# Three moves in the order of a hybrid decoder layer on one core: the decay stage against the first products of the pairs, the logarithms against the exponentials, and which PSUM bank three stages take first

## The chip, the cores and the metric

The kernel runs on one core of a Trainium2 chip. The metric is device time in microseconds. A core has five engines that work side by side, each through its own queue in program order: TensorE multiplies matrices (PE in the profile, with PEld for its loads of the stationary operand), VectorE (DVE) and ScalarE (ACT) work on elements, GpSimd (POOL) does a few operations on elements, and SyncE (SP) issues the transfers between HBM and the on-chip memory SBUF. Matrix products land in PSUM, of whose banks the kernel uses eight, each 128 partitions by 512 float32. An engine waits for another by semaphore.

## The reference

One layer of a decoder with two token mixers side by side. The input x has 1024 rows of 1024. What is computed, cut to its core:

```python
h = rmsnorm(x, norm_g)
proj = h @ w_in
(g_q, g_k, g_v, g_gate, g_rank,
 s_q, s_k, s_v, s_gate, m_logits) = jnp.split(proj, SPLIT_IDX, axis=-1)
log_a = jax.nn.log_sigmoid((g_rank @ w_dec_up + b_dec).astype(jnp.float32)) / GLA_TAU
o_gla = gla_chunked(g_q, g_k, g_v, log_a)          # 4 heads, chunks of 64
...
bcum = jnp.cumsum(la, axis=3)                      # in each chunk
qe = qc * jnp.exp(bcum) * (dk ** -0.5)
ke = kc * jnp.exp(-bcum)
...
o_sb = stick_breaking(s_q, s_k, s_v)               # 8 heads
y_a = (rmsnorm(o_gla, gla_norm_g) * silu(g_gate)) @ w_pa
y_b = (o_sb * silu(s_gate)) @ w_pb
merged = gates[0] * y_a + gates[1] * y_b           # gates = sigmoid(m_logits + b_gate)
return rmsnorm(x + merged @ w_o, final_g)
```

The decay is the part between `g_rank` (16 columns of the projection) and the two tables exp(bcum) and exp(-bcum), of four heads with 128 channels by 1024 tokens each.

## The kernel before

Every product of float32 is made of three: an operand is split into a high half, rounded to the format in which TensorE runs at full rate, and a low half, the difference; high by high, high by low and low by high are added up in PSUM. `split` (L160, L161) is two operations: ScalarE copies to the high half, VectorE subtracts to get the low half. In the names of the profile these are `wh` and `wl` (or `dh` and `dl`).

The projection is cut into jobs of 256 columns of the weights, and each job is computed with seven block products in place of eight (`pair_job`). A job has a load of the weights (L235, 1 MB, on SyncE's queue, into `raw`), four subtractions of GpSimd (L239 to L242) that make the sums T1 to T4 of weight blocks in the single buffer `tt`, four splits (B11 and B21; T2 and T1; B22; T3 and T4), and seven units. A unit is one product: twelve matmuls (L265 to L267) of 512 columns. The seven products use three banks "pp", called x, y and z. Units 0, 2, 4 and 6 go onto x, unit 1 onto y, units 3 and 5 onto z. Between them the banks are read: ScalarE copies x away after units 0 and 2 and z after unit 3 (`keep`, L271), and VectorE adds such a copy to a bank at units 1, 4 and 5 (`evict`, in `total` L304). So unit 4 cannot begin before ScalarE has copied x after unit 2, and unit 6 not before VectorE has made the addition of unit 4.

`Pairs.run(n)` (L79) issues the next n units of all jobs in one row: it issues the split that is due (the current job's last one at unit 0, the next job's others at units 2, 4 and 6), at unit 1 the load of the job after next, and then the unit. Units are counted here through all jobs from 0, so that unit 13 is unit 6 of the second job.

Ahead of the pairs stands the v stage (L676 to L678): 56 items of six matmuls with a row of constants of their own, with four banks `vx` (two of the tag "z" and two of the tag "tr", L660) that the items take in turn. Just ahead of it the column constants are transposed into a "tr" bank (`vcol_ps`, L156) and copied out by VectorE (L157). Two later stages have four such banks `xa` and `xb`.

The decay stage runs between the first units of the pairs, in a list `djobs` (L804): one entry of decay operations, then `pairs.run(1)`. For half the tokens `code` (L769) transposes the codes on TensorE into a "tr" bank and ScalarE (L706) and VectorE (L708) split them. For a head `logit` is two matmuls into "tr" banks (L776) with an addition by VectorE each (L777); `decay_a` (VectorE, L781) takes the negative magnitude, `decay_b` (ScalarE, L784) its exponential, `decay_c` (ScalarE, L787) the logarithm of one plus that, `decay_d` (VectorE, L790) a subtraction, `decay_e` (VectorE, L793) the running sum in chunks as a scan, `decay_f` (ScalarE, L796 and L797) two exponentials, and `decay_g` (VectorE, L800, and two stores, L801 and L802) hands the tables over. An operation on a head is 128 by 1024. Between exponential and logarithm ScalarE loads another table of functions (ACT_TABLE_LOAD). The list has 23 entries, the first of them empty.

The stage is under a manual schedule for ScalarE and VectorE: these two keep the order in which the code is written, while TensorE, GpSimd and SyncE are put in order by the planner. Behind the decay stage 40 units run with a list `tjobs` beside them (L841): loads, sums and stores of matrices for later (`t_load`, L829 and L832), at places counted from the start of that list.

## Time and profile before

| | |
|---|---|
| runs of before | 1189.11, 1189.91, 1189.92 us; median 1189.91 |
| the profiled execution's own time | 1189.16 us |
| its span | 1187.5 us |
| mean granted clock of TensorE in it | 0.995 of full speed |
| TensorE busy | 1165.4 us in 5811 matmuls |
| VectorE, ScalarE, GpSimd busy | 861.3, 553.6, 248.1 us |
| v stage starts, first unit of the pairs starts | 44.27 us, 102.64 us |
| first transposes of the codes, last exponential of the decay stage | 105.41 us, 175.79 us |

The profile is of one execution. Its span runs from the first to the last instruction; what lies around it, 1.7 us, is in the time and not in the span. Busy time is summed over all instructions of an engine, so a wait shows as the difference to the span. A row of the timeline has the start, the duration, the engine, the line, and what is written from what; in brackets stands how long the engine had been idle and which instruction released it.

### The profile page before, as it was taken

The numbers are of one execution on the slowest core, as the hardware profiler recorded it, in microseconds if no ns is written. First come the engines' busy times: TensorE is split into PE (matmuls) and PEld (weight loads), VectorE is DVE, ScalarE is ACT, GpSimd is POOL, SyncE is SP. The second block draws the span as 40 slices with busy tenths as digits, with TensorE's granted clock in tenths as the row PEclk, the third lists the DMA queues.
The fourth block names the chain that finished last, engine by engine and source line by source line (L and its number), as shares of the span: only waits on it lengthen the run. The fifth ranks groups of instructions, "written<-read, shape, count | busy, mean of one in ns | idle before, by whom it ended". The sixth has DMA issues, their size and how long they took to land.

```text
span 1187.5 us, 16606 instructions
## 1 busy us (share of the span) xinstructions
PE 1165.4 (98%) x5811; PEld 979.8 (83%) x5811; DVE 861.3 (73%) x1440; ACT 553.6 (47%) x1040; POOL 248.1 (21%) x217
## 2 busy tenths in 40 slices
PE   8999799999999999999999999999999999999997
PEld 7998678888888888888888887888888888888886
DVE  6797666787677777777666677447687876488986
ACT  6554562333454454454444443344444544364543
POOL 1022323234233233233233223000000000700001
PEclk9999999999999999999999999999999999999999
DMA  7324439998266565564444357899766646848652
GB/s 287 125 62 160 150 139 318 335 319 284 100 191 196 166 225 193 165 195 143 142 159 134 107 163 228 259 309 330 237 214 225 202 150 199 291 152 284 221 195 106
DMA packets 189455, 239.23 MB, mean 201 GB/s; under 512 B 12438, under 2 KB 128172, under 8 KB 187836
## 3 DMA queue, kind: packets, MB, share of 16 engines
q1 hardware_dynamic: 188796, 237.13, 60.3%
q8 instruction: 45, 0.74, 0.3%
q10 hardware_dynamic: 576, 1.05, 0.2%
q14 instruction: 38, 0.31, 0.1%
HBM read 150.06 MB, written 88.08 MB: 201 GB/s over the span
## 4 chain that ended last, share of the span: by engine, by line
PE 89%; DVE 4%; ACT 2%; DMA 2%; issue 1%; SPq 0%; ACTq 0%; DVEq 0%
PE pp L265 16%; PE pp L267 16%; PE pp L266 16%; PE pp L199 3%; PE pp L200 3%; PE pp L201 3%; PE pp L218 2%; PE av L1106 1%; PE av L1105 1%; PE tr L1083 1%; PE av L1104 1%; PE z L1065 1%; PE z L1067 1%; PE z L1066 1%; PE xb L1472 1%
## 5 line engine op out<-in xcount | busy, mean ns | idle before, releaser
L265 PE MATMUL pp<-S,wh 128*128 128x512 f32 x372 | 147.3, 396 | 0.7 <-ACT f L271 0.7
L267 PE MATMUL pp<-S,wl 128*128 128x512 f32 x372 | 145.0, 390 | 0.0
L266 PE MATMUL pp<-S,wh 128*128 128x512 f32 x372 | 144.9, 390 | 0.0
L161 DVE TENSOR_TENSOR wl<-tt,wh 128x1024 fp32r<-128x1024 f32 x62 | 76.5, 1234 | 56.6 <-ACT wh L160 56.2
L304 DVE TENSOR_TENSOR f<-pp,f 128x512 f32<-128x512 f32 x93 | 64.1, 689 | 71.7 <-PE pp L267 64.9
L239 POOL TENSOR_TENSOR tt<-raw 128x512 f32<-128x512 f32 x31 | 45.3, 1463 | 267.3 <-DVE wl L161 244.2
L160 ACT ACTIVATE wh<-tt 128x1024 fp32r<-128x1024 f32 x62 | 65.6, 1058 | 74.7 <-PE pp L266 66.0
L271 ACT ACTIVATE f<-pp 128x512 f32<-128x512 f32 x93 | 55.1, 592 | 89.2 <-PE pp L267 85.9
L1071 DVE TENSOR_TENSOR_SCAN be<-be,m 128x128 f32<-128x128 f32 (+3 forms) x64 | 86.2, 1349 | 6.2 <-ACT be L1068 6.1
L160 ACT ACTIVATE wh<-raw 128x1024 fp32r<-128x1024 f32 (+1 forms) x47 | 48.4, 1030 | 83.6 <-PE pp L266 46.4
L265 PEld LDWEIGHTS pp<-S,wh 128*128 128x128 f32 x372 | 70.6, 190 | 15.6 <-ACT f L271 1.6
L267 PEld LDWEIGHTS pp<-S,wl 128*128 128x128 f32 x372 | 69.8, 188 | 14.9
L266 PEld LDWEIGHTS pp<-S,wh 128*128 128x128 f32 x372 | 69.9, 188 | 13.7
L161 DVE TENSOR_TENSOR wl<-raw,wh 128x1024 fp32r<-128x1024 f32 (+1 forms) x47 | 65.2, 1388 | 16.6 <-ACT wh L160 16.1
L226 POOL TENSOR_TENSOR r<-r,nhalf 128x1 f32<-128x1 f32 x40 | 25.2, 629 | 194.2 <-DVE r L225 194.2
L1068 ACT ACTIVATE be<-z 128x384 f32<-128x384 f32 (+4 forms) x96 | 47.0, 495 | 24.0 <-PE z L1067 20.6
L1255 POOL TENSOR_TENSOR N<-A,A 128x512 f32<-128x512 f32 x4 | 6.6, 1659 | 242.9 <-DMA A<-d_osb 242.9
L265 PE MATMUL pp<-ha22h,wh 128*128 128x512 f32 x124 | 49.8, 402 | 6.3 <-DVE f L304 6.3
L267 PE MATMUL pp<-ha22h,wl 128*128 128x512 f32 x124 | 49.3, 397 | 0.0
L266 PE MATMUL pp<-ha22l,wh 128*128 128x512 f32 x124 | 49.2, 397 | 0.0
L265 PE MATMUL pp<-ha11h,wh 128*128 128x512 f32 x124 | 49.1, 396 | 0.0
L265 PE MATMUL pp<-ha12h,wh 128*128 128x512 f32 x124 | 49.0, 395 | 0.0
(528 smaller groups left out, 3394.6 us busy)
## 6 DMA issues: line engine op xcount, KB each, us to landing
raw<-in_w_in_dram SPq DMA_DIRECT2D x31, 1024.0 KB, 6.3
d_t<-t SPq DMA_DIRECT2D x16, 512.0 KB, 5.5
d_ogl<-o SPq DMA_DIRECT2D x64, 128.0 KB, 2.5
d_q<-o SPq DMA_DIRECT2D x16, 512.0 KB, 3.2
d_k<-o SPq DMA_DIRECT2D x16, 512.0 KB, 4.7
d_v<-o SPq DMA_DIRECT2D x32, 256.0 KB, 2.4
k<-d_k SPq DMA_DIRECT2D x8, 1024.0 KB, 6.1
v<-d_v SPq DMA_DIRECT2D x16, 512.0 KB, 5.4
```

The costliest lines, as they stand in the source:

```text
L160: nc.scalar.activation(hi, src, AF.Copy)
L161: eng.tensor_sub(lo, src, hi.bitcast(F32))
L199: nc.tensor.matmul(pt, whi[:, kb], h_, start=kb == 0, stop=False)
L200: nc.tensor.matmul(pt, whi[:, kb], l_, start=False, stop=False)
L239: nc.gpsimd.tensor_sub(t1, b[:, 0, 1], b[:, 0, 0])
L265: nc.tensor.matmul(pt, bh[:, j], ah[:, j], start=first and j == 0, stop=False, skip_group_check=True)
L266: nc.tensor.matmul(pt, bh[:, j], al[:, j], start=False, stop=False, skip_group_check=True)
L267: nc.tensor.matmul(pt, bl[:, j], ah[:, j], start=False, stop=j == 3, skip_group_check=True)
L271: nc.scalar.activation(t[nm], t[bank], AF.Copy)
L304: nc.vector.tensor_add(add, bank, add)
L1068: nc.scalar.activation(om[:, off + pc * w:off + (pc + 1) * w], zt[:, 0:w], AF.Sigmoid, scale=-inv_sqrt)
L1071: nc.vector.tensor_tensor_scan(rest, rest, m1[:, off:T][:, ::-1], 1.0, op0=ALU.mult, op1=ALU.max)
```

## The change

`Pairs.run` takes a list `mid` of further operations, which it issues behind the split and the load that are due and ahead of the unit. The decay stage hands its entries over in this way, where it called them itself ahead of `pairs.run(1)`. The list loses its empty first entry, so the first transposes of the codes come with the first unit, and in each half the second head's exponential and both heads' logarithms share one entry, where the logarithms had one of their own. So the list has 20 entries in place of 23. The list `tjobs` behind it becomes 43 entries long in place of 40, and its operations start three entries later, which leaves them at the same units. Three stages take the two "tr" banks ahead of the two "z" banks.

```diff
@@ class Pairs
-    def run(self, n=None):
+    def run(self, n=None, mid=()):
...
             if u == 1 and i + 2 < len(self.jobs):
                 self.jobs[i + 2]["load"]()
+            for fn, arg in mid:
+                fn(arg)
             due = self.late.pop(0) if self.late else None
             self.jobs[i]["unit"](u)
@@ hybrid_layer
-    vx = [ps.tile([P, HALF], F32, tag=tag, name="vx")[:, 0:VH] for tag in ("z", "z", "tr", "tr")]
+    vx = [ps.tile([P, HALF], F32, tag=tag, name="vx")[:, 0:VH] for tag in ("tr", "tr", "z", "z")]
...
-    djobs = [[], [(code, 0)], [(code, 1)]]
+    djobs = [[(code, 0)], [(code, 1)]]
     for h in (0, 2):
-        djobs += [[(logit, h)], [(logit, h + 1), (decay_a, h)], [(decay_b, h), (decay_a, h + 1)], [(decay_b, h + 1)],
-                  [(decay_c, h), (decay_c, h + 1)], [(decay_d, h)], [(decay_e, h), (decay_d, h + 1)],
+        djobs += [[(logit, h)], [(logit, h + 1), (decay_a, h)], [(decay_b, h), (decay_a, h + 1)],
+                  [(decay_b, h + 1), (decay_c, h), (decay_c, h + 1)], [(decay_d, h)], [(decay_e, h), (decay_d, h + 1)],
                   [(decay_f, h), (decay_e, h + 1)], [(decay_f, h + 1), (decay_g, h)], [(decay_g, h + 1)]]
...
     for jobs in djobs:
-        for fn, h in jobs:
-            fn(h)
-        pairs.run(1)
+        pairs.run(1, jobs)
...
     for k in range(8):
-        at = 4 * k
+        at = 4 * k + 3
...
-    xa = [ps.tile([P, HALF], F32, tag=tag, name="xa") for tag in ("z", "z", "tr", "tr")]
+    xa = [ps.tile([P, HALF], F32, tag=tag, name="xa") for tag in ("tr", "tr", "z", "z")]
...
-    xb = [ps.tile([P, HALF], F32, tag=tag, name="xb") for tag in ("z", "z", "tr", "tr")]
+    xb = [ps.tile([P, HALF], F32, tag=tag, name="xb") for tag in ("tr", "tr", "z", "z")]
```

The lines of the kernel after the change lie two further down from the second addition in `run` to the list `djobs`.

What ScalarE has in a row at the second exponential of the first two heads, before. `e_1349` and `e_1372` are the two heads' tables; `f_1431` is the copy of unit 6's bank, `dh_1415` the high half of B22 of the second job, and `wh_1436` that of its T3 and T4.

```order
L784 ACTIVATE e_1372<-e_1372 128x1024
L160 ACTIVATE dh_1415<-raw_1160 128x512
L566 ACTIVATE f_1431<-pp_1277 128x512
L787 ACT_TABLE_LOAD
L787 ACTIVATE e_1349<-e_1349 128x1024
L787 ACTIVATE e_1372<-e_1372 128x1024
L160 ACTIVATE wh_1436<-tt_1162 128x1024
```

The same place on ScalarE after the change, where the two heads' tables are `e_1335` and `e_1357`, the high halves `dh_1417` and `wh_1437`, and the copy of unit 6's bank `f_1434`.

```order
L786 ACTIVATE e_1357<-e_1357 128x1024
L789 ACT_TABLE_LOAD
L789 ACTIVATE e_1335<-e_1335 128x1024
L789 ACTIVATE e_1357<-e_1357 128x1024
L162 ACTIVATE dh_1417<-raw_1160 128x512
L568 ACTIVATE f_1434<-pp_1285 128x512
L162 ACTIVATE wh_1437<-tt_1162 128x1024
```

The table load and both logarithms have moved ahead of the small high half and of the copy of unit 6's bank.

Further on in ScalarE's queue, at the second exponentials of the same two heads (L796 and L797), before. `f_1453`, `f_1496` and `f_1514` are the copies of the banks of units 7, 9 and 10; `wh_1480` and `wh_1521` are high halves of the third job.

```order
L271 ACTIVATE f_1453<-pp_1440 128x512
L160 ACTIVATE wh_1480<-raw_1300 128x1024
L271 ACTIVATE f_1496<-pp_1440 128x512
L796 ACT_TABLE_LOAD
L796 ACTIVATE e_1349<-u_1348 128x1024
L797 ACTIVATE u_1348<-u_1348 128x1024
L271 ACTIVATE f_1514<-pp_1501 128x512
L796 ACTIVATE e_1372<-u_1371 128x1024
L797 ACTIVATE u_1371<-u_1371 128x1024
L160 ACTIVATE wh_1521<-tt_1302 128x1024
```

The same place after the change; the copies of the banks of units 7, 9 and 10 are `f_1456`, `f_1504` and `f_1522`, and the high halves `wh_1483` and `wh_1524`.

```order
L273 ACTIVATE f_1456<-pp_1443 128x512
L798 ACT_TABLE_LOAD
L798 ACTIVATE e_1335<-u_1334 128x1024
L799 ACTIVATE u_1334<-u_1334 128x1024
L162 ACTIVATE wh_1483<-raw_1300 128x1024
L798 ACTIVATE e_1357<-u_1356 128x1024
L799 ACTIVATE u_1356<-u_1356 128x1024
L273 ACTIVATE f_1504<-pp_1443 128x512
L273 ACTIVATE f_1522<-pp_1509 128x512
L162 ACTIVATE wh_1524<-tt_1302 128x1024
```

The exponentials of both heads now stand ahead of the copies of the banks of units 9 and 10, where the first head's stood between these two copies and the second head's behind them.

On TensorE at the start of the v stage, before: first matmuls of the second, third and fourth item. A wait for VectorE's semaphore stands in brackets as DVE_49; the bank of `vcol_ps` is that of the item which has it.

```order
L678 MATMUL vx_706<-wh_651,ha11l_209 128x384
L676 MATMUL vx_707<-wh_651,ha11h_208 128x384 [waits PE_49]
L677 MATMUL vx_707<-wl_652,ha11h_208 128x384
L678 MATMUL vx_707<-wh_651,ha11l_209 128x384
...
L678 MATMUL vx_707<-wh_651,ha11l_209 128x384
L676 MATMUL vx_708<-wh_651,ha11h_208 128x384 [waits DVE_49]
```

The same items after the change.

```order
L680 MATMUL vx_705<-wh_651,ha11l_209 128x384
L678 MATMUL vx_706<-wh_651,ha11h_208 128x384 [waits DVE_49]
L679 MATMUL vx_706<-wl_652,ha11h_208 128x384
L680 MATMUL vx_706<-wh_651,ha11l_209 128x384
```

The wait for VectorE's copy of the column constants has moved from the fourth item to the second, twelve matmuls earlier.

## The prediction

> **What bounds the kernel now.** I read the page first, then the stretches of 25 us, then the list of what each engine waited for, and last the engines' rows around the largest wait.

> ```profile
> span 1187.5 us, 16606 instructions
> PE 1165.4 (98%) x5811; PEld 979.8 (83%) x5811; DVE 861.3 (73%) x1440; ACT 553.6 (47%) x1040; POOL 248.1 (21%) x217
> PE 89%; DVE 4%; ACT 2%; DMA 2%; issue 1%; SPq 0%; ACTq 0%; DVEq 0%
> 125.00:150.00 25.00, 18.74 (x76) 14.79 (x75) 17.85 (x15) 13.10 (x15) 9.83 (x4) 0.92 0.43 165
> PE pp L265 <- DVE f L304: 6.3, 1, 6.3
> ```

> TensorE works through 98% of the span, and the chain that ended last is its own for 89%. So an edit counts by what it does to TensorE's waits and to its clock. Only 22 us are idle, and one wait holds 6.3 of them. It falls in the stretch 125 to 150 (a row of the stretches gives the length, then the busy time of PE, PEld, DVE, ACT and POOL, the granted clock, the DMA share and GB/s). Between the first stretch and the last 12 us it is the only one in which TensorE is busy for less than 20 of 25 us, and the granted clock is down to 0.92. It holds the decay stage. In the rows below a start is followed by a duration, and in brackets stand the wait ahead and its releaser.

> ```profile
> 123.55 0.39 PE L265 MATMUL pp<-ha11h,wh 128*128 128x512 f32 x1
> 126.27 0.39 PE L265 MATMUL pp<-ha12h,wh 128*128 128x512 f32 x1
> 140.17 0.61 PE L776 MATMUL tr<-rst,o 128*128 128x512 f32 x2
> 147.04 0.79 PE L265 MATMUL pp<-ha22h,wh 128*128 128x512 f32 x1 [6.26 <-DVE f L304]
> 147.63 0.63 PE L266 MATMUL pp<-ha22l,wh 128*128 128x512 f32 x1
> 148.06 0.63 PE L267 MATMUL pp<-ha22h,wl 128*128 128x512 f32 x1
> 152.33 0.80 PE L776 MATMUL tr<-rst,o 128*128 128x512 f32 x2
> 178.33 0.50 PE L265 MATMUL pp<-S,wh 128*128 128x512 f32 x1 [0.71 <-ACT f L271]
> ```

> A unit of the pairs, twelve matmuls, takes 126.27 - 123.55 = 2.72 us (0.227 each). Counting units from the first one, unit 7 starts at 123.55 and unit 13 at 147.04, after 6.26 us of waiting. Behind that wait the pitch is 0.43 a matmul (148.06 - 147.63), not 0.227, until 152.33: the unit takes 5.3 us instead of 2.72, and the start of the next piece is slow too, so about 2.9 us go to the halved clock that follows the wait. A smaller wait of 0.71 stands at unit 23. Together this is 6.26 + 2.9 + 0.71 = 9.9 us.

> What makes unit 13 wait is read backwards on the two engines that feed it.

> ```profile
> 115.13 0.60 ACT L271 ACTIVATE f<-pp 128x512 f32<-128x512 f32 x1 [2.57 <-PE pp L267]
> 123.75 0.60 ACT L566 ACTIVATE f<-pp 128x512 f32<-128x512 f32 x1 [1.36 <-PE pp L267]
> 124.36 1.28 ACT L787 ACT_TABLE_LOAD   x1
> 125.66 2.01 ACT L787 ACTIVATE e<-e 128x1024 f32<-128x1024 f32 x2
> 127.57 1.04 ACT L160 ACTIVATE wh<-tt 128x1024 fp32r<-128x1024 f32 x1
> 142.04 1.06 ACT L796 ACTIVATE e<-u 128x1024 f32<-128x1024 f32 x1 [5.07 <-DVE u L793]
> 143.13 1.06 ACT L797 ACTIVATE u<-u 128x1024 f32<-128x1024 f32 x1
> 144.09 1.04 ACT L160 ACTIVATE wh<-tt 128x1024 fp32r<-128x1024 f32 x1
> 128.64 1.23 DVE L161 TENSOR_TENSOR wl<-tt,wh 128x1024 fp32r<-128x1024 f32 x1 [5.53 <-ACT wh L160]
> 129.78 1.22 DVE L790 SCALAR_TENSOR_TENSOR e<-u,e 128x1024 f32<-128x1024 f32 x1
> 131.52 2.78 DVE L793 TENSOR_TENSOR_SCAN u<-rmask,e 128x1024 f32<-128x1024 f32 x1
> 134.22 2.25 DVE L790 SCALAR_TENSOR_TENSOR e<-u,e 128x1024 f32<-128x1024 f32 x1
> 138.64 3.37 DVE L793 TENSOR_TENSOR_SCAN u<-rmask,e 128x1024 f32<-128x1024 f32 x1
> 145.16 1.23 DVE L161 TENSOR_TENSOR wl<-tt,wh 128x1024 fp32r<-128x1024 f32 x1 [3.09 <-ACT wh L160]
> 146.30 0.68 DVE L304 TENSOR_TENSOR f<-pp,f 128x512 f32<-128x512 f32 x1
> 168.47 2.28 DVE L793 TENSOR_TENSOR_SCAN u<-rmask,e 128x1024 f32<-128x1024 f32 x1
> 129.95 2.21 POOL L239 TENSOR_TENSOR tt<-raw 128x512 f32<-128x512 f32 x1 [18.31 <-DVE wl L161]
> 132.11 3.29 POOL L241 TENSOR_TENSOR tt<-raw 128x512 f32<-128x512 f32 x1
> ```

> ScalarE's copy of unit 6's bank (123.75) waits for TensorE, and the table load, both logarithms (125.66) and the high half of T3 and T4 (127.57) queue behind it. VectorE then goes through wl, the first subtraction, the first scan, the second subtraction, a wl and the second scan, which ends at 142.01. ScalarE waits 5.07 us for it, runs two exponentials and the next high half (144.09), VectorE its low half (145.16), and only then the addition that empties unit 11's bank (146.30). Unit 13 writes that bank again.

> The VectorE rows are stretched. The same scan takes 2.28 at 168.47 and 2.78 and 3.37 here; the same subtraction 1.22 and 2.25. In these rows an operation of GpSimd and one of VectorE take turns: GpSimd's of 129.95 ends at 132.16, as the scan of 131.52 begins to work, and that of 132.11 ends only 1.1 after the scan. So beside GpSimd each of VectorE's operations here costs its own 1.1 (a scan 2.15) and a turn of about 1.15 before it.

> **The change part by part.** *Order of the decay stage.* Nothing is added or removed among the operations; the table loads stay four. Three moves act on this chain. The empty first entry goes, so every decay operation stands one unit of 2.72 us earlier. The logarithms stand directly behind the second exponential, another unit earlier and ahead of the copy of unit 6's bank, so they no longer wait for unit 6. And the splits stand ahead of the decay operations.

> Walked with the durations above, in the clock of before (unit 7 at 123.55 in both). The copy of unit 3's bank runs from 115.6, since a logit more (0.45) stands ahead of that unit; 0.5 later, the high half of T2 and T1, to 117.1; the first exponential to 118.1. VectorE does the low half and the second pair's minimum to 119.5. Then ScalarE: second exponential to 120.6, table load 1.28 to 121.9, logarithms 2.0 to 123.9, a small high half and the copy of unit 6's bank to 124.9, the high half of T3 and T4 to 125.9. Before, that ended at 128.6. VectorE: first subtraction by 126.2, the low half by 127.3, first scan by 129.5, GpSimd's first turn to 130.7, second subtraction to 131.8, GpSimd's second to 133.0, second scan to 135.1. That is 6.9 us before the 142.01 of today. ScalarE's two exponentials (142.04 and 143.13: 2.05 to the start of what follows) run to 137.2.

> *What is late next.* In the new order the copy of unit 9's bank stands behind those exponentials on ScalarE; before, it stood ahead of them. It ends at 137.8. Unit 11 writes that bank again. TensorE reaches it at 123.55 + 4 x 2.72 + 0.45 (the logits of the third head) = 134.9, so it waits 2.9 there. Adding up rows end to end overstates a little: the same addition over the rows of before puts unit 13 at 147.35 against 147.04. I take 0.3 off: **2.6 us**. The wait of unit 13 itself is gone, since the addition to unit 11's bank now follows the unit directly.

> With the second two heads the same chain begins behind unit 13's copy: copy 0.5, high half 0.96, exponential 0.96, table load 1.28, logarithms 1.92, copy of unit 14's bank 0.6, in all 6.2 us. Unit 16 needs that last copy and comes two units (5.44) after unit 13's end: with 0.2 for the releases between, it waits **0.95**. Behind it the copy of unit 17's bank and the addition to unit 18's stand behind the exponentials and a stretched scan: **0.5** at units 19 and 20 together. The fourth head's logit finds both "tr" banks still being read by VectorE's additions: **0.25**. Waits added by the order: 4.3 us. Today's 6.26 and 0.71 go, and with them the 2.9 of halved clock, if 2.6 us does not halve it.

> ```profile
> 841.93 0.50 PE L1104 MATMUL av<-afh,v 128*128 128x512 f32 x1 [1.57 <-ACT afh L160]
> ```

> The trace has a wait of 1.57 with no drop (the matmuls that follow keep their pitch) and one of 6.26 with a drop; 2.6 lies nearer to the first, so I price the drop at nothing, with 2.9 as the other bound. [...]

> [...] The row of 124.36 shows 1.28, beginning 0.01 behind the copy, with the logarithms 0.02 behind it. [...]

> *Banks of the v stage, and of the two later stages.*

> ```profile
> 45.44 0.33 PE L676 MATMUL vx<-wh,ha11h 128*128 128x384 f32 x1
> 47.52 0.33 PE L676 MATMUL vx<-wh,ha11h 128*128 128x384 f32 x1
> 46.26 0.17 DVE L157 COPY vcol<-vcol_ps 128x22 f32<-128x22 f32 x1
> 25.00:50.00 25.00, 25.00 (x186) 24.19 (x185) 17.97 (x33) 15.49 (x28) 2.12 (x4) 1.00 0.42 150
> ```

> The column constants are copied out of a "tr" bank, ending at 46.43. The item that takes this bank was the fourth (47.52, no wait) and becomes the second, which TensorE reaches at 45.44. It waits 46.43 - 45.44 and a few hundredths for the release: **1.0 us**. TensorE is busy for all of that stretch (25.00 of 25) and has no gap up to unit 13 that could take it up. The copy is last of its group on VectorE and can't come earlier. At the end of the stage the first transposes of the decay codes find their bank free earlier, but unit 0 bounds TensorE there in both. The later two stages start 30 us after "tr" is last read: nothing.

> *Transfers.* The loads of the t matrices stay at their units, but twelve instead of eight now stand on SyncE's queue ahead of the weights of the seventh job.

> ```profile
> 175.00:200.00 25.00, 24.29 (x107) 19.79 (x106) 14.29 (x17) 9.70 (x12) 11.61 (x8) 1.00 1.00 324
> 194.19 0.64 SPq L235 DMA_DIRECT2D raw<-in_w_in_dram  x1
> 218.09 1.05 ACT L160 ACTIVATE wh<-raw 128x1024 fp32r<-128x1024 f32 x1
> ```

> The weights are issued 23.9 us before they are first read. Four loads of 256 KB more are 1 MB, at the 324 GB/s of this stretch 3.2 us. The slack hides it: nothing.

> **Sum.** Removed: 6.26 + 2.9 + 0.71 = 9.9. Added: 4.3 + 1.0 = 5.3. Net -4.6, from the profiled execution's own 1189.16 to 1184.6. The median of the runs, 1189.91, is 0.75 above that execution, the lowest run 0.05 below; I go half way: **1185.0**. A difference of 0.2%, 2.4 us, is about what a measurement of this kernel can tell from no change, so faster means below 1187.5.

> **The rivals.** (a) *The clock halves after the new wait at unit 11.* For it: the one long wait of today did so, and 2.6 lies between the two lengths seen. Against it: the shorter one didn't. It costs the 2.9 of today again: 1187.9. Chance 0.20.

> (b) *GpSimd's turns fall elsewhere.* GpSimd starts when the low half of T3 and T4 is done, the very moment at which the first scan starts. If its four operations miss the second subtraction and scan, unit 11 waits 0.8: 1182.8. Chance 0.08. If GpSimd gets the first turn, the chain is a turn longer: +1.2, and about +0.6 with the second two heads: 1186.8, inside the forecast's own range.

> (c) *The wait only moves.* The copy of unit 9's bank stays behind exponentials that are no earlier, since the second scan is held up longer than I add up: then 6.26 and 2.9 stay, only at unit 11 instead of 13, and with the 1.0 of the v stage the time is 1190. Against it: 3.7 of the second scan's 6.9 us of advance would have to be lost. Chance 0.06. That the order doesn't do what it says is excluded for the logarithms: they do stand ahead of unit 6's copy.

> (d) *Slower: the seventh job's weights come late.* Unit 42 waits for them. Its price is one to one for every microsecond beyond the 23.9 of slack, and it decides the sign only when the weights land 7 us past that point (4.6 + 2.4): some 31 us behind their issue, while four more loads cost 3.2. At 33 us it gives 1185.0 + 9.1 = 1194. Chance 0.04.

> (e) *The table load costs the path more than its row.* If each of the two loads took twice the 1.28 of 124.36, units 11 and 16 would each wait 1.3 longer: 1187.6. Against it: the logarithms begin 0.02 behind the load's end. Chance 0.02. [...]

> **How the numbers follow.** Forecast 0.60 at 1185.0; its own bounds are 1183 and 1187. Range 1182.6 to 1188.6: it takes in (a), (b) and (e) with some tenths on each side, and leaves out (c) and (d). Faster: forecast 0.60, (b) 0.08 and a third of (a) 0.07, 0.75. Within 0.2%: the rest of (a) 0.13, (c) 0.06 and (e) 0.02, 0.21. Slower: (d) 0.04.

> **What would show it.** The second scan of the decay ends near 136 on the new clock (135.1 and the 1.0 of the v stage); unit 11 shows a wait for ScalarE's copy of 2 to 3 us with full pitch behind it; unit 13 shows none. A wait of 1.0 for VectorE's copy of the constants stands near 45.4. A pitch of 0.43 behind unit 11 would make (a) right. The forecast is wrong if unit 11 waits over 4 us, if the wait near 45.4 is missing, or if a wait of over 1 us appears past 190.

## The result, and the profile after

| | before | after |
|---|---|---|
| median of the runs | 1189.92 us (1187.86 to 1193.89, 11 runs) | 1185.26 us (1182.64 to 1188.23, 11 runs) |
| ratio | | 0.9964, 95% interval 0.9951 to 0.9977 |
| profiled execution, its span | 1189.16, 1187.5 us | 1186.62, 1184.9 us |
| granted clock over the span | 0.995 | 0.995 |

The changed kernel is 4.7 us faster at the median. The list of what TensorE waited for, after the change (us in total, times, longest):

```profile
PE pp L267 <- ACT f L273: 3.8, 2, 2.8
PE vx L678 <- DVE vcol L159: 0.9, 1, 0.9
```

The waits of 6.3 for VectorE and 0.7 for ScalarE in the decay stage are gone; two for ScalarE's copies of banks and one in the v stage have come. The stretches of the v stage and the decay stage (length; busy PE, PEld, DVE, ACT, POOL; clock, DMA share, GB/s):

```profile
25.00:50.00 25.00, 24.11 (x183) 22.98 (x182) 17.94 (x33) 16.45 (x29) 2.39 (x5) 1.00 0.43 153
...
125.00:150.00 25.00, 22.18 (x92) 17.94 (x91) 21.55 (x20) 14.09 (x17) 10.81 (x4) 0.93 0.47 171
150.00:175.00 25.00, 24.05 (x105) 19.06 (x104) 16.80 (x15) 17.35 (x20) 7.56 (x5) 1.00 0.59 204
```

TensorE's rows at these places:

```profile
47.92 0.44 PE L678 MATMUL vx<-wh,ha11h 128*128 128x384 f32 x1 [0.89 <-DVE vcol L159]
...
137.02 0.61 PE L778 MATMUL tr<-rst,o 128*128 128x512 f32 x2
140.45 0.79 PE L267 MATMUL pp<-S,wh 128*128 128x512 f32 x1 [2.82 <-ACT f L273]
141.04 0.63 PE L268 MATMUL pp<-S,wh 128*128 128x512 f32 x1
141.47 0.63 PE L269 MATMUL pp<-S,wl 128*128 128x512 f32 x1
...
147.84 0.39 PE L267 MATMUL pp<-ha22h,wh 128*128 128x512 f32 x1
...
157.10 0.50 PE L267 MATMUL pp<-S,wh 128*128 128x512 f32 x1 [0.94 <-ACT f L273]
```

Unit 11 waits 2.82 us, unit 13 (147.84) not at all, unit 16 0.94. Behind the wait of unit 11 the pitch is 0.43: the clock did halve. VectorE and ScalarE ahead of unit 11:

```profile
129.97 2.28 DVE L795 TENSOR_TENSOR_SCAN u<-rmask,e 128x1024 f32<-128x1024 f32 x1
132.17 2.26 DVE L792 SCALAR_TENSOR_TENSOR e<-u,e 128x1024 f32<-128x1024 f32 x1
134.46 3.27 DVE L795 TENSOR_TENSOR_SCAN u<-rmask,e 128x1024 f32<-128x1024 f32 x1
137.77 1.06 ACT L798 ACTIVATE e<-u 128x1024 f32<-128x1024 f32 x1 [2.38 <-DVE u L795]
138.86 1.06 ACT L799 ACTIVATE u<-u 128x1024 f32<-128x1024 f32 x1
139.82 1.07 ACT L273 ACTIVATE f<-pp 128x512 f32<-128x512 f32 x2
```

The second scan ends at 137.73, the two exponentials follow, and then the copies of two banks, the first of which (unit 9's) lets unit 11 begin. This is the chain of the prediction, operation by operation.

### The profile page after: what moved, and what is told of

Same layout as the page of the kernel before. It is cut to its first block, busy times and chain, and to the rows that moved or that the text cites. A ratio compares the mean times of both kernels' runs of the same rounds, so it can differ in the third digit from the quotient of the medians.

```text
span 1184.9 us, 16601 instructions
## 1 busy us (share of the span) xinstructions
PE 1166.4 (98%) x5811; PEld 980.8 (83%) x5811; DVE 860.6 (73%) x1440; ACT 554.1 (47%) x1040; POOL 249.2 (21%) x217
## 3 DMA queue, kind: packets, MB, share of 16 engines
q10 hardware_dynamic: 576, 1.05, 0.2%
## 4 chain that ended last, share of the span: by engine, by line
PE 90%; DVE 4%; DMA 2%; ACT 2%; issue 1%; SPq 0%; ACTq 0%; DVEq 0%
PE pp L267 16%; PE pp L268 16%; PE pp L269 16%; PE pp L203 3%; PE pp L202 3%; PE pp L201 3%; PE pp L220 2%; PE tr L1083 2%; PE z L1065 1%; PE av L1104 1%; PE av L1106 1%; PE av L1105 1%; PE z L1067 1%; PE z L1066 1%; PE xb L1471 1%; PE xb L1472 1%
## 5 line engine op out<-in xcount | busy, mean ns | idle before, releaser
L267 PE MATMUL pp<-S,wh 128*128 128x512 f32 x372 | 147.8, 397 | 3.8 <-ACT f L273 3.8
L241 POOL TENSOR_TENSOR tt<-raw 128x512 f32<-128x512 f32 x31 | 44.3, 1427 | 260.4 <-DVE wl L163 240.9
L267 PEld LDWEIGHTS pp<-S,wh 128*128 128x128 f32 x372 | 70.9, 191 | 18.8 <-ACT f L273 4.6
L163 DVE TENSOR_TENSOR wl<-raw,wh 128x1024 fp32r<-128x1024 f32 (+1 forms) x47 | 62.8, 1336 | 15.9 <-ACT wh L162 15.4
L267 PE MATMUL pp<-ha11h,wh 128*128 128x512 f32 x124 | 49.2, 397 | 0.0
L267 PE MATMUL pp<-ha12h,wh 128*128 128x512 f32 x124 | 49.1, 396 | 0.0
L242 POOL TENSOR_TENSOR tt<-raw,tt 128x512 f32<-128x512 f32 x31 | 49.0, 1581 | 0.0
L267 PE MATMUL pp<-ha22h,wh 128*128 128x512 f32 x124 | 48.8, 394 | 0.0
L267 PE MATMUL pp<-S,dh 128*128 128x512 f32 x124 | 48.7, 393 | 0.0
```

What stands on the lines that cost most here:

```text
L163: eng.tensor_sub(lo, src, hi.bitcast(F32))
L241: nc.gpsimd.tensor_sub(t1, b[:, 0, 1], b[:, 0, 0])
L242: nc.gpsimd.tensor_sub(t2, b[:, 1, 1], t1)
L267: nc.tensor.matmul(pt, bh[:, j], ah[:, j], start=first and j == 0, stop=False, skip_group_check=True)
```

## The experiments

The diffs are against the kernel before or the changed kernel, as named. In each kernel the list behind the decay stage is moved by as many entries as the decay list is shorter, so that its operations stay at their units. Beside each median stands the ratio to the kernel before, from runs on the same chip in turn with it.

### The banks alone, and the banks put back

The kernel before with the new banks of the v stage, and the changed kernel with the old ones:

```diff
-    vx = [... for tag in ("z", "z", "tr", "tr")]
+    vx = [... for tag in ("tr", "tr", "z", "z")]
```

> The kernel before, with only the v stage's banks in the new order. Both theories on the decay stage expect it unchanged. The banks bring a wait of 0.9 to 1.0 us at the second item of the v stage and nothing else: 0.9 above the kernel before, the wait of unit 13 still 6.3. If the new order were needed for the first codes, the first units would come earlier than in the kernel before, by up to 0.9, and the sum would be zero.

> The changed kernel, with the banks of the v stage alone put back (z, z, tr, tr). Theory of a trade: the wait of 0.9 us for VectorE's copy of the constants at the second item of the v stage goes, but with no empty first entry the first transposes of the codes now come to a 'tr' bank that VectorE still reads for the v stage, and TensorE waits 1.1 to 1.7 us there; the decay stage behind it shows the same waits as the changed kernel (about 2.8 at unit 11, 0.9 at unit 16). Time 0.2 to 0.8 us above the changed kernel. Rival: the bank order only brought the wait of 0.9, nothing appears at the transposes, time 0.9 below the changed kernel.

The banks alone: 1190.08 us, 1.0002 (0.9993 to 1.0011). What TensorE waited for:

```profile
PE pp L265 <- DVE f L304: 6.3, 1, 6.3
...
PE vx L676 <- DVE vcol L157: 0.9, 1, 0.9
```

The wait of unit 13 is untouched and the 0.9 has come; units 0 to 12 start 1.07 later than in the profile of before; the interval of the ratio is too wide to tell 0.9 us from nothing. The banks put back: 1183.63 us, 0.9947 (0.9932 to 0.9962), 1.6 below the changed kernel at the median; the two intervals overlap, so here too the traces decide and not the times. Its profile has no wait near 45 us and none at the transposes of the codes either, and the waits of units 11 (2.81) and 16 as before. So the theory of a trade fell and the rival held: in the traces the new banks of the v stage cost 0.9 us and bring nothing. The transposes of the first half come behind unit 0 on TensorE there (unit 1 starts 0.35 later than in the kernel before and unit 4 0.08 earlier), when their bank is free. The new order of the banks `xa` and `xb` was not run by itself; TensorE's one wait in those two stages (0.5 at L1350) is the same before and after.

### One move of the decay stage at a time

Each on the kernel before, with the old banks. The empty entry taken out:

```diff
-    djobs = [[], [(code, 0)], [(code, 1)]]
+    djobs = [[(code, 0)], [(code, 1)]]
```

> The kernel before, with only the empty first entry of the decay list taken out (and the later list moved by one, so that its operations stay at their units): no splits ahead, logarithms in their own entry, old banks. Theory that the three moves of the decay stage are not a sum but each a shift of one chain against the copies of the banks: one unit earlier is enough, the copies of units 9, 10 and 14 stay ahead of the exponentials and logarithms that would hold them, and the waits of the stage fall from 7.1 us to about 0.9 (0.2 and 0.4 at the logits of the third and fourth head, 0.3 at unit 20), with no halved clock in the stage: 1179.5 to 1181.5, that is 4 us below the whole change. Rival (the moves add up; the entry alone gives a third): a wait of 2 us or more at unit 11 to 13, time 1184 or more.

The splits ahead (the decay operations handed to `run` and issued behind the split and the load):

```diff
     for jobs in djobs:
-        for fn, h in jobs:
-            fn(h)
-        pairs.run(1)
+        pairs.run(1, jobs)
```

> The kernel before, with only the splits and the load issued ahead of the decay operations: 23 entries with the empty one, logarithms in their own entry, old banks. The same theory: four waits of 0.3 to 1.3 us (0.5 at unit 9, 0.5 at unit 13, 0.3 at unit 20, 1.3 at unit 23), 2.7 together, none long enough to halve the clock: 1181 to 1183. Rival (the moves add up): the wait of unit 13 shrinks only by the splits' own time, some 2 us, and stays above 3.

The logarithms merged into the entry of the second exponential:

```diff
-        ... [(decay_b, h + 1)],
-        [(decay_c, h), (decay_c, h + 1)], [(decay_d, h)], ...
+        ... [(decay_b, h + 1), (decay_c, h), (decay_c, h + 1)], [(decay_d, h)], ...
```

> The kernel before, with only the logarithms merged into the entry of the second exponential (22 entries with the empty one; no splits ahead, old banks). Theory that each move is a shift of the decay's chain against the copies of the banks: four waits in place of 6.3 and 0.7: 1.4 at unit 12 for ScalarE's copy of unit 10's bank, 0.8 and 0.4 at the logits of the third and fourth head, 2.0 at unit 20 for VectorE's addition; 4.6 together, hardly a halved clock: 1182.5 to 1185. Rival (moves add up; the splits ahead and the entry taken out bring 7 and 8 us, so the merging must cost them back): slower than the kernel before, with a wait of over 6.3 in the stage.

The entry alone: **1179.31 us**, 0.9912 (0.9898 to 0.9925). The splits alone: 1182.20, 0.9938 (0.9926 to 0.9951). The logarithms alone: 1183.76, 0.9959 (0.9947 to 0.9972). Each of them is faster than the kernel before. The entry alone is also clearly faster than the whole change (its interval lies below 0.9951 to 0.9977); the splits alone are so too, by intervals that just touch, and the logarithms alone cannot be told from the whole change. In the profile of the entry alone TensorE is busy for 24.84 of the 25 us in which before it was for 18.74:

```profile
125.00:150.00 25.00, 24.84 (x109) 20.04 (x109) 21.73 (x20) 15.41 (x19) 12.73 (x6) 1.00 0.61 218
```

ScalarE's rows show why. Unit 9's copy, the second head's exponentials and unit 10's copy stand in this order:

```profile
131.83 0.60 ACT L271 ACTIVATE f<-pp 128x512 f32<-128x512 f32 x1
134.18 1.07 ACT L796 ACTIVATE e<-u 128x1024 f32<-128x1024 f32 x1 [1.76 <-DVE u L793]
135.28 1.06 ACT L797 ACTIVATE u<-u 128x1024 f32<-128x1024 f32 x1
136.25 0.58 ACT L271 ACTIVATE f<-pp 128x512 f32<-128x512 f32 x1
```

Unit 9's bank is copied at once, and the exponentials wait for their scan when no unit waits for them. In the changed kernel that copy stands behind them. The time of the entry alone lies 0.2 below the range expected, the other two lie in theirs. The waits came close to what was expected: 0.15 and 0.17 with the entry out; 0.45, 0.17, 0.28 and 0.93 with the splits ahead; 1.07, 0.44, 0.16 and 1.86 with the logarithms merged.

### Two moves together

The entry out and the logarithms merged, on the kernel before:

> The kernel before, with the empty entry out and the logarithms merged, but no splits ahead and old banks. Two moves that are each good alone: by the theory of shifts the first two heads run without a wait, but with the second two the same pile-up as in the kernel before appears: 1.0 at unit 16 and about 6 us at unit 20 for VectorE's addition, with a halved clock of one or two windows: 1187 to 1190.5, no better than the kernel before. Rival (moves add up, or the gain of the entry alone stays): 1180 or less.

The changed kernel with its logarithms in an entry of their own again, that is the entry out and the splits ahead (with the new banks):

```diff
-                  [(decay_b, h + 1), (decay_c, h), (decay_c, h + 1)], [(decay_d, h)], [(decay_e, h), (decay_d, h + 1)],
+                  [(decay_b, h + 1)], [(decay_c, h), (decay_c, h + 1)], [(decay_d, h)], [(decay_e, h), (decay_d, h + 1)],
```

> The changed kernel, with the logarithms of a pair of heads in an entry of their own again, behind the split and the copy of the next unit's bank. Theory that the place of the logarithms sets what waits: the wait of unit 11 goes, since the second scan comes later and the exponentials stand behind the copy of unit 9's bank; unit 12 waits about 4.5 us for ScalarE's copy of unit 10's bank behind the exponentials, followed by a halved clock; no wait at unit 16, one of about 1.1 at unit 20. Time 2 to 4 us above the changed kernel. Rival (the gain comes from the splits ahead and the entry taken out, the merged entry gives nothing): waits and time as in the changed kernel within 0.5 us.

The first: 1187.90 us, 0.9986 (0.9977 to 0.9995). Its TensorE rows:

```profile
149.86 0.50 PE L265 MATMUL pp<-S,wh 128*128 128x512 f32 x1 [0.94 <-ACT f L271]
...
167.76 0.79 PE L265 MATMUL pp<-ha22h,wh 128*128 128x512 f32 x1 [5.78 <-DVE f L304]
```

The first two heads run without a wait, and the second two show at unit 20 what the kernel before shows at unit 13. The second kernel: 1189.17 us, 0.9998 (0.9987 to 1.0010), with 4.21 at unit 12. ScalarE's rows there:

```profile
135.17 0.58 ACT L273 ACTIVATE f<-pp 128x512 f32<-128x512 f32 x1
140.80 1.06 ACT L798 ACTIVATE e<-u 128x1024 f32<-128x1024 f32 x1 [5.05 <-DVE u L795]
141.89 1.06 ACT L799 ACTIVATE u<-u 128x1024 f32<-128x1024 f32 x1
142.85 0.58 ACT L273 ACTIVATE f<-pp 128x512 f32<-128x512 f32 x1
```

Here unit 10's copy (142.85) is the one caught behind the exponentials, which wait 5.05 us for their scan. So the entry and the logarithms, 10 and 5 us alone, bring 1.1 together at the median, and the entry and the splits, 10 and 7 alone, nothing (0.9 of it for the banks). The third pair, the splits and the logarithms, was not run. The moves don't add up: each shifts the decay's chain by some microseconds against the copies of the banks, and what counts is which copy gets caught.

### The copies ahead

The changed kernel with banks tr, z, z, tr, and with the logarithms and the second head's last exponentials issued behind their unit:

```diff
+            for fn, arg in post:
+                fn(arg)
...
+                  ([(decay_b, h + 1)], [(decay_c, h), (decay_c, h + 1)]), ([(decay_d, h)], []),
...
+                  ([(decay_g, h)], []), ([], [(decay_f, h + 1), (decay_g, h + 1)])]
```

> The changed kernel, with the banks of the v stage as tr, z, z, tr, and with the logarithms and the second head's last exponentials issued behind their unit, so that the copies of the banks of units 9, 10 and 14 stand ahead of them on ScalarE. Theory that ScalarE's order alone makes the remaining waits: no wait above 0.3 us at units 11 to 23 and none near 45 us, at most 0.3 at the codes, no halved clock in the decay stage; waits of about 5 us less than in the changed kernel, and the halved clock of up to 1.8 besides: 1178.5 to 1180.5. Rival (the chain's length decides, the wait moves on to the addition ahead of unit 13 or to a low half): a wait of 2 us or more at unit 12 or 13, time 1183 or more.

1180.87 us, 0.9924 (0.9909 to 0.9939). No wait at 45 us, at the codes or at units 11 and 16. The edit changes the banks and the order together. The wait at 45 us belongs to the banks, since it goes with the banks put back too; those of units 11 and 16 stay there (2.81 and 0.94) and are gone here, so ScalarE's order made them. But there is a wait of 2.28 at unit 19, so the time is 0.4 above the range expected:

```profile
157.16 1.06 ACT L800 ACTIVATE e<-u 128x1024 f32<-128x1024 f32 x1 [3.09 <-DVE u L797]
158.25 1.06 ACT L801 ACTIVATE u<-u 128x1024 f32<-128x1024 f32 x1
159.21 0.58 ACT L275 ACTIVATE f<-pp 128x512 f32<-128x512 f32 x1
```

The first head's exponentials of the second pair were left where they stood, and now unit 17's copy is the one behind them.

### GpSimd's turns

The changed kernel with GpSimd's subtractions of the third job held back until the second scan is done. In both tries the decay operations also stand ahead of the load at unit 1, so that the next job's sums come behind the held ones. The first try copied a column of the scan into a tile of its own:

```diff
+    held = const.tile([P, 1], F32, tag="held", name="held")
...
+        if h == 1:
+            nc.gpsimd.tensor_copy(held, U[h][:, T - 1:T])
+            held_subs.pop()()
```

> The changed kernel, with GpSimd's four subtractions of the third job held back until the second head's scan is done (by a copy of one column of it). Theory of turns (an operation of GpSimd and one of VectorE with two inputs in SBUF run only one after the other): the second subtraction takes 1.2 instead of 2.26 and the second scan 2.3 instead of 3.27, the scan ends about 2.2 earlier, and unit 11 waits 0.5 to 0.8 us instead of 2.8, too short for the clock to halve; time 3 to 4 us below the changed kernel. Rival (the stretch comes from elsewhere, or the end of the exponentials is set by something other than the scan): the rows stay at 2.3 and 3.3 or the wait of unit 11 stays above 2 us.

It did not hold anything back: the order put the copy behind the subtractions, which ran as ever, and the second head's second exponential on ScalarE waited 2.39 for the copy besides (4.60 at unit 11). It also took 1205.45 us, with every unit at 2.80 us. The second try writes into the subtractions' own output first:

```diff
+                if after is not None:
+                    nc.gpsimd.tensor_copy(tt[:, :, 0, 0], after[:, T - 4:T])
```

> The changed kernel, with GpSimd's four subtractions of the third job held back until the second head's scan is done: a copy of four columns of it goes into their output first, and no tile is added (the earlier try had a one-column tile more, and the planner put the copy behind the subtractions). Theory of turns: second subtraction 1.2 instead of 2.26, second scan 2.3 instead of 3.27, unit 11 waits 0.5 to 0.8 instead of 2.8, no halved clock in the stage, 2 to 4.5 us below the changed kernel; a pitch of 2.72 a unit, where the earlier try had 2.80 throughout. Rival: rows and wait as in the changed kernel. If the pitch stays at 2.80, it was not the added tile.

VectorE's second subtraction and second scan in it:

```profile
130.59 1.20 DVE L803 SCALAR_TENSOR_TENSOR e<-u,e 128x1024 f32<-128x1024 f32 x1
131.82 2.29 DVE L806 TENSOR_TENSOR_SCAN u<-rmask,e 128x1024 f32<-128x1024 f32 x1
```

TensorE's two waits in the same kernel:

```profile
136.89 0.50 PE L278 MATMUL pp<-S,wh 128*128 128x512 f32 x1 [0.84 <-ACT f L284]
...
142.49 0.50 PE L789 MATMUL tr<-rst,o 128*128 128x512 f32 x1 [2.11 <-DVE u L790]
```

Without GpSimd beside them the subtraction takes 1.20 and the scan 2.29, as elsewhere, and unit 11 waits 0.84 in place of 2.82. So GpSimd's operations cost 2.0 us of that wait. The time didn't follow (1185.54, 0.9962, 0.9950 to 0.9975): the sums of the next job come later, VectorE's low half for them stands ahead of the third head's addition, and the fourth head's logit, which needs the bank that this addition reads, waits 2.11 for it, with a window of halved clock behind it (0.50 from 143.74 to 147.16).

### Four bytes

The changed kernel with a tile of one column more among the constants, and a memset of it:

```diff
+    spare = const.tile([P, 1], F32, tag="spare", name="spare")
+    nc.gpsimd.memset(spare, 0.0)
```

> The changed kernel with one column of 4 bytes a partition more among the constants, and a memset of it. If that tile alone made the earlier try slow: 2.80 us a unit in place of 2.72 in the pairs, some 1203 to 1206. If not: 2.72 and the changed kernel's time.

1201.86 us in one run, span 1200.2. The first matmuls of units 7 and 8:

```profile
126.23 0.40 PE L267 MATMUL pp<-ha11h,wh 128*128 128x512 f32 x1
...
129.03 0.40 PE L267 MATMUL pp<-ha12h,wh 128*128 128x512 f32 x1
```

2.80 us a unit, where the changed kernel has 2.72. So it was the tile: the first try above had such a tile too, filled by a copy, and ran at 2.80; the second try had none and ran at 2.72. The time is 1.1 below the range expected.

## Why the prediction was right, and where it was not

| step | forecast, us | measured |
|---|---|---|
| wait of unit 13 goes, wait of unit 23 goes | -6.26, -0.71 | -6.26, -0.71 |
| halved clock behind unit 13 goes | -2.9 | -2.8 (unit 13 took 5.93 with a logit of 0.45, and 2.72 are its own) |
| end of the second scan, in the clock of before | 135.1 | 137.73 - 2.59 = 135.14 |
| wait at unit 11 | 2.6 | 2.82 |
| wait at unit 16 | 0.95 | 0.94 |
| units 19 and 20 | 0.5 | 0.3, and 0.15 more at unit 21 (starts 162.72, 165.53, 168.42, 171.29 at a pitch of 2.72; none long enough to be listed as a wait) |
| fourth head's logit | 0.25 | none |
| v stage | 1.0 | 0.9, and 1.07 with the banks alone |
| halved clock behind unit 11 | none | 1.5 (unit 11 took 4.19) in the profiled execution |
| time | 1185.0 | 1185.26 |

**The chain and the sum of its waits were right.** The order of the engines' queues, with durations from the rows of before, gave each new wait its place and its length. The one step that failed is the clock. The prediction took it that a wait's length decides and priced 2.6 us at nothing, as nearer to 1.57 than to 6.26; rival (a) had it at 2.9. In the profiled execution it halved, which by the prediction's own sign, the pitch of 0.43 behind unit 11, is rival (a), but for half its price. The last section shows that the length alone doesn't decide. The profiled execution, 1186.62, stands 2.0 above the forecast of 1184.6 for it: 1.5 of this is that window, and 1.45 another at the start, which before's profile didn't have (the v stage begins at 45.72, not 44.27, ahead of anything that the change touches); 0.8 comes back later (the changed kernel is 1.74 ahead at unit 42 and 2.55 at the end of the span; the wait of 1.57 at L1104 does not occur in its profile). The granted clocks suggest that such windows fell in some runs and not in others: the fastest of the eleven (1182.64) had a granted clock of 0.999, those from 1186.62 up 0.994 or 0.995. So it is in part luck that the median came within 0.3 us of the forecast: the sum leaves out a term of 1.5 that fell in the profiled execution, and whether it fell in the median run is not known.

**The rivals.** (b) was right in its price: with the turns out of the way unit 11 waits 0.84, where it said 0.8. (c) did not happen; its price of 1190 leaves out terms of the prediction's own sum (1.7 for the other new waits, 0.71 that goes) and comes to about 1191 with them. Nor did (d): the seventh job's weights are issued at 192.02 and read at 216.34, 24.3 us later, and unit 42 follows unit 41 at the full pitch, 2.72 us. (e): the load takes 1.28 and the logarithms start 0.02 behind it, so the row held, and nothing was added to it.

**What the prediction did not see** was not in its sum: that the change takes a good move and spends most of it. Taking out the empty entry alone gains 10 us; the splits ahead on top, with the new banks, bring that back to nothing, and the merged logarithms mend 4 us of it. The prediction worked out the three moves as one shift of the chain and never asked what the first alone would give.

## What to carry to other kernels

When two chains share an in-order queue, moving one of them earlier has a best place, not a direction: ask for each move which operation, with a consumer waiting, now stands behind one that itself waits. Work out the single moves as well as their sum. And give a wait's cost as its length plus the chance that it takes a window of halved clock with it (here 1.5 us behind the 2.82 of unit 11, and none behind the 2.28 of unit 19 with the copies ahead).

## What the runs showed of the hardware that was not expected

```profile
139.05:142.46 3.41, 1.73 (x8) 1.11 (x6) 3.02 (x2) 0.42 (x1) 0.81 (x1) 1.00 0.00 0
142.46:145.88 3.42, 0.00 (x0) 0.00 (x0) 0.72 (x1) 3.16 (x4) 0.00 (x0) 1.00 0.59 242
145.88:149.29 3.41, 2.25 (x5) 1.82 (x6) 3.41 (x7) 0.00 (x0) 0.00 (x0) 0.50 0.56 219
149.29:152.71 3.42, 3.42 (x9) 2.64 (x8) 0.29 (x1) 0.14 (x1) 0.00 (x0) 0.50 0.54 151
```

Two windows of the changed kernel, the one ahead of the drop and the halved one:

```profile
136.51:139.92 3.41, 1.13 (x5) 0.59 (x4) 3.41 (x4) 2.12 (x3) 3.33 (x2) 1.00 0.30 119
139.92:143.34 3.42, 2.89 (x7) 2.31 (x8) 2.69 (x4) 1.91 (x3) 1.10 (x1) 0.50 0.71 290
```

The window ahead of the drop in the changed kernel with the old banks:

```profile
135.83:139.24 3.41, 1.47 (x6) 1.24 (x7) 2.68 (x4) 3.29 (x5) 2.43 (x2) 1.00 0.84 341
```

The same in the second try with held subtractions:

```profile
140.33:143.74 3.41, 1.30 (x6) 1.05 (x6) 3.29 (x5) 0.09 (x1) 0.37 (x1) 1.00 0.00 0
```

Windows in which TensorE was busy for 0, 1.13, 1.30 or 1.47 us were followed by half the clock, one with 1.73 was not. Out of the halved state, 2.25 were not enough and 2.89 were. Busy time alone does not decide, though. At the start of the changed kernel 1.85 us were followed by half the clock, which is the other window of the account above, while 1.62 in the kernel with four bytes more (138.51 to 141.92) were not:

```profile
10.22:13.63 3.41, 1.85 (x12) 1.37 (x11) 2.51 (x5) 2.76 (x6) 1.53 (x1) 1.00 1.05 412
13.63:17.04 3.41, 3.41 (x18) 3.41 (x17) 2.14 (x4) 1.29 (x3) 0.55 (x1) 0.50 1.03 402
```

So of two waits of nearly one length, 1.98 and 2.09 us, one was followed by half the clock and the other not. The same matmul shows it in two kernels. With the banks alone its wait lies within one window, which is followed by half the clock:

```profile
843.63 0.69 PE L1104 MATMUL av<-afh,v 128*128 128x512 f32 x1 [1.98 <-ACT afh L160]
840.36:843.77 3.41, 1.43 (x8) 0.92 (x6) 1.33 (x4) 1.88 (x4) 0.00 (x0) 1.00 0.88 311
843.77:847.18 3.41, 3.41 (x14) 3.15 (x14) 3.14 (x6) 2.64 (x7) 0.00 (x0) 0.50 0.86 244
```

With the splits alone a slightly longer wait lies across two windows, and the clock stays:

```profile
835.12 0.51 PE L1104 MATMUL av<-afh,v 128*128 128x512 f32 x1 [2.09 <-ACT afh L162]
830.34:833.76 3.42, 2.69 (x20) 2.18 (x18) 1.99 (x4) 1.42 (x4) 0.00 (x0) 1.00 0.88 242
833.76:837.17 3.41, 2.00 (x12) 1.67 (x12) 2.56 (x5) 3.41 (x9) 0.00 (x0) 1.00 0.79 271
```

Waits of 2.28 (the copies ahead) and 2.25 (four bytes) did not halve it in their profiles either, those of 2.82, 2.81 and 2.11 did. What in a window decides was not tried.

**GpSimd and VectorE take turns** in the operations seen here, which read two operands from SBUF each: 2.26 against 1.20 and 3.27 against 2.29 for the same operations of VectorE with GpSimd's beside them and without. That one waits for the other, and not both slow down, shows in the first try with held subtractions: a scan that begins at 128.79 takes its 2.28, and GpSimd's subtraction of 128.95 takes 3.22, where such a subtraction takes 1.29 with VectorE idle (before, at 194.49). Whether operations with one operand do the same was not tried.

**Four bytes a partition among the constants** put the matmuls of the pairs 0.233 us apart in place of 0.227 and made the kernel 16.6 us slower than the changed kernel's median, in one run. That the tiles allocated behind the constants all lie 4 bytes further is a guess; no run shows what in the added tile did it.
